# A constant tile multiplied ahead of the first data, and a last tile finished in two parts by two engines

## The chip, the cores and the metric

The kernel is one program on 1 core of one Trainium2 chip. Its metric is the device time of one execution in microseconds. The core has five engines that run side by side, each through its own list of instructions in order: TensorE (PE in the profile: matrix products; PEld are its weight loads), VectorE (DVE), ScalarE (ACT), GpSimd (POOL) and SyncE (SP), which here issues DMAs. They wait for each other through semaphores.

## The reference, cut to what matters

One layer of a decoder, on a prompt of 1024 rows of width 1024, and on eight single-row samples with a paged cache of 8192 positions. The sample group's work is spread between the prompt's. All data are float32.

```python
q, k, v, logf, u, z = mixer_inputs(rmsnorm(xp, g_mix[l]), w_in[l], b_f[l], g_sgu_v[l])
xp = xp + merge_heads(fox_prompt(q, k, v, logf), sgu_prompt(u, z, w_s[l], b_s[l]), g_att_out[l], g_sgu_out[l], w_o[l])
mk, mv = memory_kv(mem_prompt, g_mem[l], w_ck[l], w_cv[l])
xp = xp + cross_attend(rmsnorm(xp, g_cross[l]), mk, mv, w_cq[l], w_co[l])
f, conv_p = conv_ffn(rmsnorm(xp, g_ffn[l]), zeros, w_up[l], conv_w[l], conv_b[l], w_down[l])
xp = xp + f
...
y_prompt = rmsnorm(xp, g_final)
y_sample = rmsnorm(xs, g_final)

def rmsnorm(x, g):
    y = x * rsqrt(mean(x * x, axis=-1) + EPS)
    return y * g
```

What the change touches is the very start (before the first product of `mixer_inputs`) and the very end (`xp + f` and the final `rmsnorm` of the prompt's last 128 rows).

## The kernel before, in words

The prompt's 1024 rows are worked in two halves (`hf` 0 and 1) of 512, each as four tiles of 128 rows (`i` 0 to 3). A float32 product is made of three passes over operands split into a high and a low part of type float32r (`split`, lines 232 to 239: ACT writes the high part, DVE the rest): `gemm3` (lines 268 to 274) issues high times high, high times low, low times high. A plain float32 matmul (sample rows, transposes) goes without the split and is recorded as two or more passes.

**Order.** The program is written as generators whose steps are interleaved, and the Tile framework then places all instructions with a scheduler that runs a timeline model (`schedule_with_timeline_sim=True`, line 2003). So the order of an engine's list is the scheduler's: an instruction more at the start can move others far behind it. `tc.high_priority()` puts a step ahead of others that are ready.

**The start.** Constants are set by DVE (`ones`, `mhalf`, `epsb`, lines 180 to 185). SP issues the loads of `xT` and `w_in` (`load_x` line 388, `wload` line 252), four chunks of 256 of the contraction each, through four raw buffers (`wr`). In `p1` PE first multiplies the samples' rows by the raw weights (`sample_mm`, line 306), then the prompt's by the split ones (`by_rows`, lines 479 to 481), chunk by chunk. `MS()` (line 152) is one PSUM bank of its own.

**The end.** In `ffn` the down projection runs in groups of columns of the hidden width (`GROUPS`, 6, 6, 5, 5). Of the last group, for each half `n` of the 1024 output columns and each row tile `i`, `gemm3` makes 15 matmuls of 512 columns, and `residual` (line 1012) adds the result to `xt[i]` on DVE (line 1016) and sums its squares on ACT (`ssq_into`, line 230) into `sq[:, i, n]`. `final` (line 1346) then takes tile by tile: DVE adds the two halves' sums (line 1021) and scales them (222), POOL raises to the power -0.5 (223), DVE multiplies the tile by that factor and by `g_final` in one instruction (1353), SP issues the store to `o_y` (1354). The last tile of each half is multiplied and stored in two pieces of 512 columns.

Of the kernel before, what the change touches and what calls it, by code (L numbers as in the profile page):

```python
# [11 lines left out]
AF = mybir.ActivationFunctionType  # L12
ALU = mybir.AluOpType
# [5 lines left out]
P = 128  # L19
D = 1024  # L20
# [10 lines left out]
NF = FF // P  # L31
# [47 lines left out]
def build(nc, tc, ctx, a, phases=None):  # L79
# [27 lines left out]
    def nm(s):  # L107
        cnt[0] += 1
        return f"{s}_{cnt[0]}"
# [16 lines left out]
    def sm(shape, tag, bufs=2, dt=F32):  # L126
        return small.tile(shape, dt, tag=tag, bufs=bufs, name=nm(tag))
# [13 lines left out]
    def BB():  # L141
        return psum.tile([P, 512], F32, tag="bb", bufs=2 + MB, name=nm("bb"))
# [7 lines left out]
    MM = TR = BK  # L150

    def MS():
        return BB() if MB else psum.tile([P, 512], F32, tag="ms", bufs=1, name=nm("ms"))
# [11 lines left out]
    mmul = nc.tensor.matmul  # L165
# [14 lines left out]
    ones = const.tile([P, P], F32, tag="ones", name="ones")  # L180
    nc.vector.memset(ones, 1.0)
    mhalf = const.tile([P, 8], F32, tag="mhalf", name="mhalf")
    nc.vector.memset(mhalf, -0.5)
    epsb = const.tile([P, 1], F32, tag="epsb", name="epsb")
    nc.vector.memset(epsb, EPS)
    warm = const.tile([P, 1], F32, tag="warm", name="warm")
    nc.scalar.activation(warm, mhalf[:, 0:1], AF.Copy)
    bfb = const.tile([P, 8], F32, tag="bfb", name="bfb")
# [29 lines left out]
    def rstd_of(ssq, n, width, tag):  # L218

        p = ssq.shape[0]  # L220
        r = sm([P, width], tag + "r", 2)[:p]
        nc.vector.tensor_scalar(r, ssq, 1.0 / n, EPS, op0=ALU.mult, op1=ALU.add)
        nc.gpsimd.tensor_tensor(r, r, mhalf[:p, :width], op=ALU.pow)
        return r

    def ssq_into(dst, src):
        n = src.shape[-1]

        j = src if n > 512 else tpool.tile([P, 512], BF16, tag="junk", bufs=1, name=nm("junk"))[: src.shape[0], :n]
        nc.scalar.activation(j, src, AF.Square, accum_out=dst)  # L230
# [21 lines left out]
    def wload(src, n, raw=None):  # L252

        if raw is None:
            raw = wraw(src, n)
        l = spool.tile([P, SWID], F32R, tag="wl", bufs=WL, name=nm("wl"))[:, :n]
        h = spool.tile([P, SWID], F32R, tag="wh", bufs=WH, name=nm("wh"))[:, :n]
        if len(src.shape) == 3:
            h = h.rearrange("p (a b) -> p a b", b=src.shape[2])
            l = l.rearrange("p (a b) -> p a b", b=src.shape[2])  # L260
        split(raw, h, l)
        return h, l, raw
# [5 lines left out]
    def gemm3(out, pairs):  # L268

        n = len(pairs)  # L270
        for i, (sh, sl, mh, ml) in enumerate(pairs):
            mmul(out, sh, mh, start=(i == 0), stop=False)  # L272
            mmul(out, sh, ml, start=False, stop=False)  # L273
            mmul(out, sl, mh, start=False, stop=(i == n - 1))  # L274
# [734 lines left out]
    def squares():  # L1009
        return sm([P, 4, 2], "sqx", 2)  # L1010
# [8 lines left out]
    def rows_rstd(sq, i0, i1):  # L1019
        s = sm([P, i1 - i0], f"rq{i0}", 2)  # L1020
        nc.vector.tensor_tensor(s, sq[:, i0:i1, 0], sq[:, i0:i1, 1], op=ALU.add)
        return rstd_of(s, D, i1 - i0, f"rn{i0}")
# [238 lines left out]
    def ffn(hf, xt, ys, late=None):  # L1261
        begun = {ft: (wload(a["w_up"][ft], 1024), BK()) for ft in (0,)}

        def pairs(w, hs, ls, c):
            hv, lv = (w[q].rearrange("p (k c) -> p k c", c=P) for q in range(2))
            return [(hv[:, k, :], lv[:, k, :], hs[k][:, c], ls[k][:, c]) for k in range(8)]

        def first(hs, ls, c):
            gemm3_late([(pv[:, c], pairs(w, hs, ls, c)) for w, pv in begun.values()])

        hs, ls = yield from norm_T(ys, G_FFN, first)
        if hf:

            fix = sm([P, 2 * NF, 2], "fix", 1)
            tap = [gp[:, CW + i * 44 : CW + i * 44 + 44] for i in range(2)]
            for c in range(2):
                nc.vector.tensor_tensor(fix[:, :, c], hlast[0][:, :, 1], tap[1 - c], op=ALU.mult)
            t = sm([P, 2 * NF], "fixt", 1)
            nc.vector.tensor_tensor(t, hlast[0][:, :, 0], tap[0], op=ALU.mult)
            nc.vector.tensor_tensor(fix[:, :, 0], fix[:, :, 0], t, op=ALU.add)  # L1280
        sq = squares()
        f0 = 0
        for gi, gn in enumerate(GROUPS):
            gh, gl = [], []
            for f in range(f0, f0 + gn):
                hc2 = []
                for part in range(2):
                    ft = f + part * NF
                    cw = [gp[:, CW + i * 44 + ft : CW + i * 44 + ft + 1] for i in range(3)]
                    cb = gp[:, CB + ft : CB + ft + 1]  # L1290
                    if ft in begun:
                        pv = begun.pop(ft)[1]
                    else:
                        w_, pv = wload(a["w_up"][ft], 1024), BK()
                        gemm3(pv, pairs(w_, hs, ls, slice(0, 512)))
                    hc = T2()
                    nc.scalar.activation(hc, pv, AF.Identity, bias=cb, scale=cw[2])
                    nc.scalar.activation(hlast[hf][:, ft, :], pv[:, 510:512], AF.Copy)
                    nc.vector.scalar_tensor_tensor(hc[:, 1:], pv[:, :511], cw[1], hc[:, 1:], op0=ALU.mult, op1=ALU.add)
                    nc.vector.scalar_tensor_tensor(hc[:, 2:], pv[:, :510], cw[0], hc[:, 2:], op0=ALU.mult, op1=ALU.add)  # L1300
                    if hf:
                        nc.vector.tensor_tensor(hc[:, 0:2], hc[:, 0:2], fix[:, ft, :], op=ALU.add)
                    hc2.append(hc)
                    yield 5.2
                nc.scalar.activation(hc2[0], hc2[0], AF.Silu)
                nc.vector.tensor_tensor(hc2[1], hc2[1], hc2[0], op=ALU.mult)
                q = (f - f0) % 2
                if q == 0:
                    g2, l2 = U([P, 2, 512], F32R), U([P, 2, 512], F32R)
                split(hc2[1], g2[:, q, :], l2[:, q, :])  # L1310
                gh.append(g2[:, q, :])
                gl.append(l2[:, q, :])
            side = None
            if late and f0 + gn == NF:
                side = late()
            for n in range(2):
                ws = []
                for k2 in range(0, gn, 2):
                    m = min(2, gn - k2)
                    r0 = (f0 + k2) * P  # L1320
                    h, l, _ = wload(
                        a["w_down"][r0 : r0 + m * P, n * 512 : (n + 1) * 512].rearrange("(k p) n -> p k n", p=P), m * 512
                    )
                    for q in range(m):
                        ws.append((h[:, q, :], l[:, q, :]))
                for i in range(4):
                    tb = slice(i * P, (i + 1) * P)
                    ps = MM()
                    gemm3(ps[:, :512], [(gh[k][:, tb], gl[k][:, tb], ws[k][0], ws[k][1]) for k in range(gn)])
                    if f0 + gn < NF:  # L1330
                        xs_ = xt[i][:, n * 512 : (n + 1) * 512]
                        nc.vector.tensor_tensor(xs_, ps[:, :512], xs_, op=ALU.add)
                    else:
                        residual(xt, sq, i, n, ps)
                    yield 3.9
                    if side and n:

                        held[0] = True
                        for _ in range(2):
                            yield next(side)  # L1340
            f0 += gn
        if hf:
            nc.sync.dma_start(a["o_h"], hlast[1])
        return sq

    def final(hf, xt, sq):
        gf = U([P, D])
        nc.sync.dma_start(gf, a["g_final"].broadcast_to((P, D)))
        for i in range(4):
            r = rows_rstd(sq, i, i + 1)  # L1350
            rows = slice((hf * 4 + i) * P, (hf * 4 + i + 1) * P)
            for c in (slice(0, 512), slice(512, D)) if i == 3 else (slice(0, D),):
                nc.vector.scalar_tensor_tensor(xt[i][:, c], xt[i][:, c], r, gf[:, c], op0=ALU.mult, op1=ALU.mult)
                nc.sync.dma_start(a["o_y"][rows, c], xt[i][:, c])
        yield 1

    lastexp = []
    last = {}
    bgs, acc, phase = [], [0.0], ["p1", None]

# [664 lines left out]
```

## Time and profile before

| | |
|---|---|
| time, median of 3 runs | 1793.09 us (1792.41 to 1802.47) |
| the profiled execution, its own time | 1796.66 us |
| its span, first to last instruction | 1794.9 us |
| PE busy | 1736.6 us of the span, 9637 matmul records |
| DVE, ACT, POOL busy | 1399.3, 734.4, 496.1 us |
| moved by DMA | 521.07 MB, mean 290 GB/s |

The span is read along PE, which is busy nearly throughout: what counts are the stretches in which it is not, or in which its clock is low. Matmuls overlap in the records, so the pace is read from the distance of their starts, not from their durations.

### The profile page before, as it was taken

Reading aid. Unit: us, or ns where it says so; the run is one execution under the profiler, and the core shown is the slowest. Engines: PE = TensorE matmul, PEld = TensorE weight load, DVE = VectorE, ACT = ScalarE, POOL = GpSimd, SP = SyncE. Lnnn points to the kernel's source line nnn. Section 1 sums busy time; section 2 is a strip of 40 time slices with the busy share of each in tenths; the row PEclk is TensorE's granted clock in tenths of the full one; section 3 lists DMA queues with packets and bytes.
Section 4 is the critical chain, followed back from the end, with each engine's and each line's share of the span. In section 5 each row is a group of like instructions: output and inputs, shape, how many; then the busy total and the mean of one; then the engine's idle time right before and its main releaser. Section 6 shows DMA issues by size and latency. Waiting matters only on the chain.

```text
span 1794.9 us, 25099 instructions
## 1 busy us (share of the span) xinstructions
PE 1736.6 (97%) x9637; PEld 1286.9 (72%) x9637; DVE 1399.3 (78%) x1733; ACT 734.4 (41%) x1374; POOL 496.1 (28%) x461
## 2 busy tenths in 40 slices
PE   8999999889999999999999999999999999999997
PEld 5887777655677667777777777776676778767875
DVE  4689658988788987999999999887885549855344
ACT  6332256466643635333333244335353233333332
POOL 1252334432222332233322223333322122102110
PEclk9999999999999999999999999999999999999999
DMA  8886888787697975779788878978879687568982
GB/s 299 304 295 222 301 324 318 260 274 230 254 401 279 366 300 222 287 289 349 293 304 311 289 309 318 382 292 331 312 288 343 221 301 250 192 259 299 358 311 81
DMA packets 157075, 521.07 MB, mean 290 GB/s; under 512 B 20874, under 2 KB 40842, under 8 KB 124186
## 3 DMA queue, kind: packets, MB, share of 16 engines
q0 software_dynamic: 57168, 341.14, 50.2%
q1 hardware_dynamic: 92874, 165.73, 26.6%
q10 hardware_dynamic: 6912, 12.59, 1.9%
q8 instruction: 76, 1.25, 0.3%
q14 instruction: 45, 0.37, 0.1%
HBM read 495.47 MB, written 23.93 MB: 289 GB/s over the span
## 4 chain that ended last, share of the span: by engine, by line
PE 53%; DMA 9%; issue 8%; DVE 6%; POOL 2%; ACT 2%; POOLq 0%; DVEq 0%; ACTq 0%; SPq 0%
DMA kv<-cache_v,io 7%; PE ba L272 6%; PE ba L274 6%; PE ba L273 6%; PE dv L1488 4%; PE bb L272 3%; PE bb L273 3%; PE bb L274 3%; PE ba L1065 1%; PE ba L1064 1%; PE ba L1066 1%; PE dv L331 1%; DVE kv L1436 1%; PE dv L1764 1%; DVE s L1440 1%
## 5 line engine op out<-in xcount | busy, mean ns | idle before, releaser
L235 ACT ACTIVATE wh<-wr 128x1024 fp32r<-128x1024 f32 (+2 forms) x220 | 228.7, 1044 | 438.9 <-PE ba L273 152.7
L236 DVE TENSOR_TENSOR wl<-wr,wh 128x1024 fp32r<-128x1024 f32 (+2 forms) x220 | 263.0, 1200 | 165.7 <-PE ba L274 58.0
L1420 POOL DMA_INDIRECT kv<-cache_k,io x128 | 188.8, 1475 | 589.2 <-DVE s L1440 317.7
L1436 DVE TENSOR_TENSOR kv<-kv,d 128x1024 f32<-128x1024 f32 (+1 forms) x156 | 258.0, 1681 | 25.0 <-DMA kv<-cache_k,io 25.0
L1440 DVE TENSOR_REDUCE s<-kv 128x16 f32<-128x1024 f32 (+1 forms) x156 | 258.4, 1673 | 0.0
L1482 POOL DMA_INDIRECT kv<-cache_v,io x128 | 168.7, 1318 | 243.2 <-PE dv L1488 155.6
L272 PE MATMUL ba<-u,wh 128*128 128x512 f32 x528 | 209.8, 398 | 0.0
L273 PE MATMUL ba<-u,wh 128*128 128x512 f32 x528 | 208.8, 395 | 0.5 <-DVE u L239 0.5
L274 PE MATMUL ba<-u,wl 128*128 128x512 f32 x528 | 209.2, 397 | 0.0
L272 PE MATMUL ba<-wh,u 128*128 128x512 f32 (+1 forms) x495 | 186.1, 379 | 0.9 <-ACT u L235 0.9
L273 PE MATMUL ba<-wl,u 128*128 128x512 f32 (+1 forms) x495 | 185.3, 375 | 1.5 <-DVE wl L236 1.5
L274 PE MATMUL ba<-wh,u 128*128 128x512 f32 (+1 forms) x495 | 183.2, 375 | 0.0
L1488 PE MATMUL dv<-kv,s 128*32 128x512 f32 x1024 | 126.5, 600 | 4.6 <-DMA kv<-cache_v,io 4.6
L274 PEld LDWEIGHTS ba<-u,wl 128*128 128x128 f32 x528 | 99.5, 188 | 28.3 <-issue 5.7
L272 PEld LDWEIGHTS ba<-u,wh 128*128 128x128 f32 x528 | 99.6, 189 | 26.6 <-issue 4.8
L273 PEld LDWEIGHTS ba<-u,wh 128*128 128x128 f32 x528 | 99.6, 189 | 25.1 <-issue 2.3
L272 PEld LDWEIGHTS ba<-wh,u 128*128 128x128 f32 x495 | 93.0, 188 | 25.0 <-issue 6.5
L272 PE MATMUL bb<-u,wh 128*128 128x512 f32 x272 | 108.6, 399 | 0.0
L273 PE MATMUL bb<-u,wh 128*128 128x512 f32 x272 | 107.9, 397 | 0.1
L274 PE MATMUL bb<-u,wl 128*128 128x512 f32 x272 | 107.9, 397 | 0.0
L273 PEld LDWEIGHTS ba<-wl,u 128*128 128x128 f32 x495 | 93.1, 188 | 20.7 <-DVE wl L236 2.5
L274 PEld LDWEIGHTS ba<-wh,u 128*128 128x128 f32 x495 | 92.9, 188 | 19.4 <-issue 1.6
(451 smaller groups left out, 3311.9 us busy)
## 6 DMA issues: line engine op xcount, KB each, us to landing
wr<-w_up SPq DMA_DIRECT2D x88, 512.0 KB
kv<-w_up POOLq DMA_DIRECT2D x22, 1024.0 KB
wr<-w_down SPq DMA_DIRECT2D x40, 512.0 KB
kv<-w_down POOLq DMA_DIRECT2D x11, 1024.0 KB
wr<-w_in SPq DMA_DIRECT2D x16, 512.0 KB
wr<-w_o SPq DMA_DIRECT2D x16, 512.0 KB
wr<-w_cq SPq DMA_DIRECT2D x16, 512.0 KB
wr<-w_co SPq DMA_DIRECT2D x16, 512.0 KB
```

Source lines behind the costliest of these rows:

```text
L235: nc.scalar.activation(h, src, AF.Copy)
L236: nc.vector.tensor_tensor(l, src, h.bitcast(F32), op=ALU.subtract)
L272: mmul(out, sh, mh, start=(i == 0), stop=False)
L273: mmul(out, sh, ml, start=False, stop=False)
L274: mmul(out, sl, mh, start=False, stop=(i == n - 1))
L331: mmul(ps[32 * j : 32 * j + 32, :w], xT[:, k, :] if nk == 8 else xT[:, k * 8 : k * 8 + 32], raw[:, q, j * w : (j + 1) * w], start=(k == 0) ...
L1064: mmul(pss[i], mh[k][:, tb], wh, start=(k == korder[0]), stop=False)
L1420: nc.gpsimd.indirect_dma_start(kv, None, a["cache_k"], off(kidx[:, b, ch : ch + 1]))
L1436: nc.vector.tensor_tensor(kvv[:, i : i + m, :], kvv[:, i : i + m, :], qb.unsqueeze(1).broadcast_to((P, m, 512)), op=ALU.mult)
L1440: nc.vector.tensor_reduce(s[:, ch * 4 + i : ch * 4 + i + m, :].rearrange("p k h -> p (k h)"), kvv[:, i : i + m, :].rearrange("p k (h d) -> ...
L1482: nc.gpsimd.indirect_dma_start(kv, None, a["cache_v"], off(kidx[:, b, ch : ch + 1]))
L1488: mmul(dv[32 * j : 32 * j + 32, :], s[:, ch * 4 : ch * 4 + 4, :].rearrange("p k h -> p (k h)"), kvv[:, j, :], start=(ch == 1), stop=(ch == ...
```

## The change

It has two parts, in the lines below (numbers of the new file are 3 higher behind line 186, and 39 higher at the end).

1. Behind the constants, 13 float32 matmuls of the 128x128 tile `ones` with itself, into the PSUM bank of `MS()`. Nothing reads the result.
2. In the second half of the rows the last tile of the last group (`i == 3`, `n == 1`) goes to a new function `last_tile`: two products of 256 columns each, each with its own add and sum of squares, the mean and epsilon folded into ACT's instructions, so that DVE's two small steps fall away ahead of POOL's power. In `final`, tiles 2 and 3 of the second half are multiplied by two engines: columns 0 to 511 by `g_final` on DVE ahead of time and by the factor on ACT, columns 512 to 1023 by both on DVE; tile 3's first piece is stored from ACT's queue, the other pieces from SP's.

```diff
+    wm = MS()
+    for _ in range(13):
+        mmul(wm[:, :P], ones, ones, start=True, stop=True)
...
+        def last_tile(x, sq, pairs):
+            c2 = sm([P, 2], "lsq", 1)
+            part = sm([P, 2], "lpart", 1)
+            r3 = sm([P, 1], "lr", 1)
+            nc.scalar.activation(part[:, 0:1], sq[:, 3, 0:1], AF.Identity, scale=1.0 / D, bias=epsb)
+            for m in range(2):
+                ps = MM()
+                c = slice(m * 256, m * 256 + 256)
+                gemm3(ps[:, :256], [(sh, sl, mh[:, c], ml[:, c]) for sh, sl, mh, ml in pairs])
+                xs_ = x[:, 512 + m * 256 : 768 + m * 256]
+                with tc.high_priority():
+                    nc.vector.tensor_tensor(xs_, ps[:, :256], xs_, op=ALU.add)
+                    ssq_into(c2[:, m : m + 1], xs_)
+                    nc.scalar.activation(
+                        r3 if m else part[:, 1:2], c2[:, m : m + 1], AF.Identity, scale=1.0 / D, bias=part[:, m : m + 1]
+                    )
+            nc.gpsimd.tensor_tensor(r3, r3, mhalf[:, 0:1], op=ALU.pow)
+            lastr.append(r3)
...
+                    if hf and n and i == 3 and f0 + gn == NF:
+                        last_tile(xt[3], sq, [(gh[k][:, tb], gl[k][:, tb], ws[k][0], ws[k][1]) for k in range(gn)])
+                        continue
...
+            if hf and i > 1:
+                r = lastr[0] if i == 3 else rows_rstd(sq, i, i + 1)
+                for n, c in enumerate((slice(0, 512), slice(512, D))):
+                    if n:
+                        nc.vector.scalar_tensor_tensor(xt[i][:, c], xt[i][:, c], r, gf[:, c], op0=ALU.mult, op1=ALU.mult)
+                        nc.sync.dma_start(a["o_y"][rows, c], xt[i][:, c])
+                    else:
+                        nc.vector.tensor_tensor(xt[i][:, c], xt[i][:, c], gf[:, c], op=ALU.mult)
+                        nc.scalar.activation(xt[i][:, c], xt[i][:, c], AF.Copy, scale=r)
+                        (nc.scalar if i == 3 else nc.sync).dma_start(a["o_y"][rows, c], xt[i][:, c])
+                continue
```

The scheduler also places other instructions anew. On PE the order differs here and there from the 23rd row of its list to about the 3150th of 7049 (roughly the first 800 us), then not again until the last tile; DVE, ACT, POOL and SP likewise. Three places follow; names are those of the tiles (with the buffer's number), sizes are partitions by elements.

**PE at the start, before.** `wr` are raw weights, `xg` the samples' rows, `wh`, `wl` and `u` the split weights and rows.

```order
L2003 UNCONDITIONAL_BRANCH
L306 MATMUL ba_128<-wr_137,xg_108 32x512 x2
L479 MATMUL bb_275<-wh_140,u_131 128x512
L479 MATMUL ba_276<-wh_140,u_131 128x512
L479 MATMUL ba_277<-wh_140,u_131 128x512
L479 MATMUL bb_278<-wh_140,u_131 128x512
L480 MATMUL bb_275<-wl_139,u_131 128x512
```

And in the changed kernel:

```order
L2042 UNCONDITIONAL_BRANCH
L188 MATMUL ms_92<-ones 128x128 x13
L309 MATMUL ba_142<-wr_151,xg_122 32x512 x2
L482 MATMUL bb_289<-wh_154,u_145 128x512
L482 MATMUL ba_290<-wh_154,u_145 128x512
L482 MATMUL ba_291<-wh_154,u_145 128x512
L482 MATMUL bb_292<-wh_154,u_145 128x512
L483 MATMUL bb_289<-wl_153,u_145 128x512
```

The 13 new matmuls stand first; what follows them is as before. The samples' next pair, which stood three matmuls ahead of the end of the first chunk, now stands behind it.

**PE in the first half's attention, before** (scores `ba`: lines 807 to 811; transposes of weights `wr` by `cp`: line 836; values `bb_3775`: line 852).

```order
L852 MATMUL bb_3775<-u_3587,u_3212 64x256
L807 MATMUL ba_3809<-u_3566,u_3562 128x320
L809 MATMUL ba_3809<-u_3567,u_3562 128x320
L807 MATMUL ba_3809<-u_3566,u_3562 128x320
L809 MATMUL ba_3809<-u_3567,u_3562 128x320
L811 LDWEIGHTS ident_b
L811 MATMUL ba_3809<-cmask_b,ident_b 128x128
L836 MATMUL ms_3745<-cp,wr_3690 128x128 x4
L807 MATMUL ba_3828<-u_3566,u_3562 128x384
```

And now (lines 3 higher, buffers 14 higher):

```order
L855 MATMUL bb_3789<-u_3601,u_3226 64x256
L855 MATMUL bb_3789<-u_3691,u_3226 64x256
L855 MATMUL bb_3789<-u_3602,u_3226 64x256
L839 MATMUL ms_3810<-cp,wr_3747 128x128 x4
L810 MATMUL ba_3823<-u_3580,u_3576 128x320
L812 MATMUL ba_3823<-u_3581,u_3576 128x320
```

Of the value matmuls into that bank only one stood ahead of the two blocks of scores (`ba_3809`, `ba_3828`); now nine stand there, with groups of transposes between them.

**DVE and ACT at the end, before.** First DVE, then ACT; `u_9507` is tile 2, `u_9509` tile 3 (in the new file `u_9521` and `u_9523`).

```order
L1016 TENSOR_TENSOR u_9507<-ba_14727,u_9507 128x512
L1353 TENSOR_SCALAR u_9505<-u_9505,rn1r_14777,u_14766 128x1024
L1021 TENSOR_TENSOR rq_2654_14782<-sqx_11168 128x1
L222 TENSOR_SCALAR rn2r_14784<-rq_2654_14782 128x1
L1353 TENSOR_SCALAR u_9507<-u_9507,rn2r_14784,u_14766 128x1024
L1016 TENSOR_TENSOR u_9509<-bb_14746,u_9509 128x512
L1021 TENSOR_TENSOR rq_2656_14789<-sqx_11168 128x1
L222 TENSOR_SCALAR rn3r_14791<-rq_2656_14789 128x1
L1353 TENSOR_SCALAR u_9509<-u_9509,rn3r_14791,u_14766 128x512 x2
```

```order
L230 ACTIVATE junk_14669,sqx_11168<-u_9509 128x512
L230 ACTIVATE junk_14706,sqx_11168<-u_9503 128x512
L230 ACTIVATE junk_14725,sqx_11168<-u_9505 128x512
L230 ACTIVATE junk_14744,sqx_11168<-u_9507 128x512
L230 ACTIVATE junk_14763,sqx_11168<-u_9509 128x512
```

And now, DVE first:

```order
L1019 TENSOR_TENSOR u_9521<-ba_14741,u_9521 128x512
L1391 TENSOR_SCALAR u_9519<-u_9519,rn1r_14817,u_14806 128x1024
L1024 TENSOR_TENSOR rq_2660_14822<-sqx_11182 128x1
L1298 TENSOR_TENSOR u_9523<-bb_14764,u_9523 128x256
L225 TENSOR_SCALAR rn2r_14824<-rq_2660_14822 128x1
L1382 TENSOR_SCALAR u_9521<-u_9521,rn2r_14824,u_14806 128x512
L1298 TENSOR_TENSOR u_9523<-ba_14784,u_9523 128x256
L1382 TENSOR_SCALAR u_9523<-u_9523,lr_14762,u_14806 128x512
```

```order
L233 ACTIVATE junk_14758,sqx_11182<-u_9521 128x512
L233 ACTIVATE junk_14781,lsq_14760<-u_9523 128x256
L1300 ACTIVATE lpart_14761<-lsq_14760,lpart_14761 128x1
L1386 ACTIVATE u_9521<-u_9521,rn2r_14824 128x512
L233 ACTIVATE junk_14801,lsq_14760<-u_9523 128x256
L1300 ACTIVATE lr_14762<-lsq_14760,lpart_14761 128x1
L1386 ACTIVATE u_9523<-u_9523,lr_14762 128x512
L1387 DMA o_y<-u_9523 128x512
```

DVE's work of 1024 columns on tile 2 ahead of tile 3's add has become one of 512, and the two small steps behind that add are gone; ACT has three instructions between the two sums of squares and the store. The two multiplications by `g_final` (line 1385 of the new file) stand earlier in DVE's list.

More of the change, by code (lines that the diff above doesn't have):

```diff
@@ L1349, in final @@
         for i in range(4):
+            rows = slice((hf * 4 + i) * P, (hf * 4 + i + 1) * P)
+            if hf and i > 1:
[9 more added lines that the diff above has]
+                continue
             r = rows_rstd(sq, i, i + 1)
-            rows = slice((hf * 4 + i) * P, (hf * 4 + i + 1) * P)
             for c in (slice(0, 512), slice(512, D)) if i == 3 else (slice(0, D),):
@@ L1357, in build @@
     lastexp = []
+    lastr = []
     last = {}
```

## The prediction

> **What bounds the kernel now.** I read the page's first lines, then a table of PE's busy time in wide stretches, then the first 23 us and the last 13 us instruction by instruction, and last the stretches in which PE's clock is low.
>
> ```profile
> span 1794.9 us, 25099 instructions
> PE 1736.6 (97%) x9637; PEld 1286.9 (72%) x9637; DVE 1399.3 (78%) x1733; ACT 734.4 (41%) x1374; POOL 496.1 (28%) x461
> ```
>
> The table's first column behind the stretch is its length, then PE's busy time and matmul records, the other engines, PE's granted clock, the DMA share and GB/s.
>
> ```profile
> 0.00:100.00 100.00, 91.66 (x545) 74.63 (x546) 59.39 (x80) 47.04 (x72) 21.17 (x22) 1.00 0.81 297
> 300.00:800.00 500.00, 471.29 (x2631) 343.08 (x2630) 436.51 (x612) 249.27 (x524) 159.46 (x154) 0.99 0.80 290
> 1755.00:1794.90 39.90, 30.55 (x148) 22.95 (x140) 19.35 (x37) 8.74 (x24) 2.75 (x5) 0.93 0.18 68
> ```
>
> PE is the bound. Of its 58.3 us without a matmul (1794.9 - 1736.6), 8.3 lie in the first 100 us, 28.7 between 300 and 800, 9.4 in the last 40. The change can win at both ends; in between it can only shift waits. Matmul records overlap, so pace is the distance of starts. The start:
>
> ```profile
> 0.83 0.17 DVE L181 MEMSET ones<- 128x128 f32 x1 [0.83 <-PEq L2000]
> 7.10 1.92 PE L306 MATMUL ba<-wr,xg 128*32 128x512 f32 x4 [7.10 <-DMA wr<-w_in]
> 8.08 1.23 DVE L236 TENSOR_TENSOR wl<-wr,wh 128x1024 fp32r<-128x1024 f32 x1 [0.17 <-ACT wh L235]
> 8.95 0.80 PE L479 MATMUL bb<-wh,u 128*128 128x512 f32 x1
> 10.83 0.59 PE L480 MATMUL bb<-wl,u 128*128 128x512 f32 x1
> 11.25 0.40 PE L481 MATMUL bb<-wh,u 128*128 128x512 f32 x1
> 14.68 0.39 PE L481 MATMUL ba<-wh,u 128*128 128x512 f32 x1
> 15.00 1.05 PE L306 MATMUL ba<-wr,xg 128*32 128x512 f32 x4
> 18.66 1.41 DVE L239 SCALAR_TENSOR_TENSOR u<-wr,gp,u 128x512 fp32r<-128x512 f32 x2
> ```
>
> The first data release PE at 7.10. Two matmuls start 0.42 us apart (10.83 and 11.25), the 15 from there to 14.68 0.229 apart; the samples' pair takes 1.92 us at first and 1.05 later. PE runs at half pace for its first 4 us. (The clock column says 1.00 in the first 100 us although the pace doubles: there I trust the pace.)
>
> **Part 1, the constant tile.** Each new matmul is a float32 product of 128x128. The same form runs here in one row of 16 records, two for each of 8 instructions:
>
> ```profile
> 341.69 1.96 PE L649 MATMUL ba<-wr,u 128*128 128x128 f32 x16
> 343.40 0.36 PE L807 MATMUL ba<-u,u 128*128 128x256 f32 x1
> ```
>
> That is (343.40 - 341.69) / 8 = 0.214 us each at full pace, twice that, 0.43, at half. PE can start when `ones` is set, at about 1.05. Thirteen at half pace end at 1.05 + 5.6 = 6.6, before the data at 7.10: they cost nothing. If the clock rises as it did before, 4 us after PE's start, that is at about 5.1; 9 or 10 are slow, the rest end near 5.9.
>
> What it wins if the clock stays up: the pair runs 7.10 to 8.1; the four high-by-high matmuls end near 9.1; then PE waits for `wl`, ready at 8.08 + 1.23 = 9.31, and goes on at 9.35. Before, five prompt matmuls had started by 11.25, where full pace began; now four are done at 9.35. So PE is ahead by 11.25 - 9.35 - 0.229 = **1.67 us**. The next loads must keep up: the third chunk's last low part is ready at 18.66 + 1.41 = 20.07, and PE wants it after 44 matmuls and one pair, at 9.35 + 10.1 + 1.3 = 20.7, so 0.6 us of cover is left. The samples' second pair, now three matmuls later in the list, still ends at about 15.1 against 16.05 before, so the raw buffer it frees, and SP's weight load that waits for it, are not late. DVE, ACT and SP are not touched; later the evacuations and `wl` follow PE, so the lead is kept.
>
> **Does the clock stay up?** PE then idles from about 5.9 to 7.10, and 0.25 us for `wl`. Four stretches of 3.4 us:
>
> ```profile
> 366.26:369.67 3.41, 1.77 (x15) 1.22 (x16) 3.38 (x6) 2.85 (x8) 1.17 (x2) 1.00 1.07 401
> 376.49:379.90 3.41, 1.52 (x11) 1.05 (x10) 3.41 (x8) 2.92 (x7) 0.00 (x0) 1.00 0.11 31
> 379.90:383.31 3.41, 3.41 (x17) 3.10 (x17) 3.41 (x7) 1.83 (x6) 1.64 (x2) 0.50 0.02 2
> 1325.40:1328.80 3.40, 2.36 (x14) 0.94 (x6) 3.40 (x8) 1.58 (x4) 2.79 (x3) 1.00 1.05 383
> ```
>
> Behind stretches with PE busy 1.77 or 1.52 of 3.41 us (52%, 45%) the clock was 0.50 for one such stretch (third row); behind 2.36 of 3.40 (69%) it stayed. From a rise at 5.1 the next 3.41 us hold 1.2 us of idle time, so the share is 65%, nearer to the last row, so I take it that the clock stays. The Trainium skill ("TensorE: Matmul & The Clock Gate", Part 1) says the clock falls only after an idle window of about 3.4 us; by that a gap of 1.2 us is safe and the gain certain. The trace disagrees: half-idle windows were enough, so I keep the fall as a rival.
>
> **Part 2, the last tile.**
>
> ```profile
> 1777.92 0.69 DVE L1016 TENSOR_TENSOR u<-bb,u 128x512 f32<-128x512 f32 x1 [5.41 <-PE bb L274]
> 1781.80 8.63 SPq L1354 DMA_DIRECT2D o_y<-u  x5
> 1781.91 0.39 PE L272 MATMUL bb<-wh,u 128*128 128x512 f32 x1
> 1784.33 0.54 POOL L223 TENSOR_TENSOR rn2r<-rn2r,mhalf 128x1 f32<-128x1 f32 x1 [1.67 <-DVE rn2r L222]
> 1784.90 1.28 DVE L1353 SCALAR_TENSOR_TENSOR u<-u,rn2r,u 128x1024 f32<-128x1024 f32 x1 [0.65 <-POOL rn2r L223]
> 1785.15 0.40 PE L274 MATMUL bb<-wh,u 128*128 128x512 f32 x1
> 1786.11 0.68 DVE L1016 TENSOR_TENSOR u<-bb,u 128x512 f32<-128x512 f32 x1
> 1786.88 0.63 ACT L230 ACTIVATE junk<-u 128x512 bf16<-128x512 f32 x1 [3.27 <-DVE u L1016]
> 1787.42 0.19 ACT L230 ACTIVATION_READ_ACCUMULATOR junk<-u 128x1 f32 x1
> 1788.07 0.55 POOL L223 TENSOR_TENSOR rn3r<-rn3r,mhalf 128x1 f32<-128x1 f32 x1 [3.20 <-DVE rn3r L222]
> 1788.65 1.42 DVE L1353 SCALAR_TENSOR_TENSOR u<-u,rn3r,u 128x512 f32<-128x512 f32 x2 [0.66 <-POOL rn3r L223]
> ```
>
> Behind PE's last matmul (1785.55) the add waits until 1786.11 for DVE, busy with tile 2; then sum, two small steps, power, two multiplications, the last store at 1790.1. For the halves these rows give prices:
>
> ```profile
> 66.11 0.28 PE L274 MATMUL bb<-wh,u 128*128 128x260 f32 x1
> 66.23 0.28 PE L272 MATMUL bb<-wh,u 128*128 128x260 f32 x1
> L1646 DVE TENSOR_TENSOR dec<-dv,dec x6: 402/414/416, 1441.0 to 1765.1; 8x256 f32<-8x256 f32 x6
> L1185 ACT ACTIVATE cbs<-cmx,rq x32: 277/284/308, 581.5 to 1259.5; 128x1 f32<-128x1 f32 x32
> ```
>
> PE: 30 matmuls of 256 at 0.12 are 3.6 us for 15 at 0.229, 3.44; PE ends at about 1785.6, the first half near 1783.9. DVE adds that half (0.41) ahead of tile 2's small step, so tile 2's power moves from 1784.33 to about 1784.7 and ends at 1785.25; its multiplication of 512 columns (0.75, half of the 1.42) runs to 1786.0, the last add to 1786.45 instead of 1786.79. Sum of squares: about 0.52 with the readout (0.73 for 512 columns, less 0.21 for half of them), to 1787.0; ACT's step of one column 0.28, to 1787.3; the power from 1787.4 to 1787.95, where 1788.62 stood. Then the two engines multiply in parallel: both pieces are ready by 1788.73 (DVE, 0.75) and near 1788.6 (ACT, 0.63 for 512 columns), instead of 1789.37 and 1790.07. `g_final`'s multiplications on DVE ahead of time cost 0.7 us each in DVE's idle 5.4 us before 1777.9, on no path. Tile 2's two stores stand ahead of tile 3's on SP and are issued by 1786.3.
>
> The stores (the last two columns are the DMA share and GB/s):
>
> ```profile
> 1790.00:1791.00 1.00, 0.00 (x0) 0.00 (x0) 0.06 (x1) 0.00 (x0) 0.00 (x0) 0.50 0.72 274
> 1791.00:1791.50 0.50, 0.00 (x0) 0.00 (x0) 0.00 (x0) 0.00 (x0) 0.00 (x0) 0.50 1.03 393
> 1791.50:1792.00 0.50, 0.00 (x0) 0.00 (x0) 0.00 (x0) 0.00 (x0) 0.00 (x0) 0.50 0.29 107
> ```
>
> 274 x 1.0 + 393 x 0.5 + 107 x 0.5 is 524 KB, both pieces of the last tile, moved without a gap to about 1791.65: the second waited for the first's bytes, not for DVE alone. So what counts is when the first piece is ready, near 1788.6 instead of 1789.37: **0.76 us** won. If the second piece alone counted, it would be 1790.07 - 1788.73 = 1.34; if ACT's and DVE's steps on the half tile cost as much as on a whole one, some 0.4. I take 0.76, the row's reading. The Trainium skill ("DMA: Bandwidth & Descriptors", Issuing engines are not separate DMA queues) says that DMAs from several engines share the same 16 DMA engines and save only issue time. That speaks against storing from ACT's queue too, and agrees with these rows; by it the term is 0.76, without it 1.34.
>
> **Part 3, the new order up to about 800 us.** Nothing is added there but moves. One place where it matters:
>
> ```profile
> 403.35 0.42 PE L807 MATMUL ba<-u,u 128*128 128x320 f32 x1 [0.68 <-ACT wr L817]
> 406.27 0.45 PE L807 MATMUL ba<-u,u 128*128 128x384 f32 x1 [1.53 <-ACT wr L817]
> ```
>
> PE waits there 0.68 and 1.53 us for ACT to empty a score bank. Now eight value matmuls stand ahead of both. If they were ready, they would fill 2.2 us; but they read what ACT and DVE write behind a transpose that now stands just ahead of them, so they may wait as long themselves. I count zero. Bounds: a low-clock stretch costs 3.41 / 2 = 1.7 us, and the idle time that sets it off 3.41 - 1.77 = 1.6; one such event more or less is 3.3 us. PE idles 28.7 us between 300 and 800, so I allow one or two events either way, about -4 to +6.
>
> **Sum.** 1.67 + 0.76 = 2.43 us, of 1796.66 for the profiled execution (span 1794.9 and 1.76 around it), that is 1794.2. That execution lies 3.57 above the median of 1793.09; against the median the forecast is **1790.7 us**.
>
> **The rivals.**
>
> *The clock falls again in the gap.* For it: if the clock rises early, say at 4.5, eight matmuls are slow and five fast, PE is done by 5.6, idles 1.5 us plus 0.25 at 9.1, and a stretch that holds most of it is 50 to 56% busy, close to the 52% that sufficed. Against: 69% did not, and the phase of these stretches decides. Then the prompt's matmuls are slow from about 8 to 11.3, as before, and only the tail is won: 1793.09 - 0.76 = 1792.3.
>
> *The new order costs: slower than before.* The mechanism is one: in the first half's attention PE waits for ACT's evacuations, and a wait that leaves a 3.4 us stretch half idle halves the clock for the next. For it: two such drops lie between 366 and 384 in the rows above already, and PE's order differs most from here to 620 us. Against: as many waits can vanish. It decides from 2.4 us on, so one new event of 3.3 us suffices: 1790.7 + 3.3 = 1794.0; two give 1797.3.
>
> *The new order wins.* The same the other way: 2.2 us of waits at 403 to 406 and the 1.7 us of one low-clock stretch gone give 1790.7 - 3.9 = 1786.8.
>
> *The tile does nothing.* If a product of ones did not raise the clock, 1792.3 again; nothing in this trace shows a matmul whose operands matter, so I put it into the first rival.
>
> **How the numbers follow.** Forecast 0.43; clock falls or never rises 0.19; order costs 0.23; order wins 0.15. The range of 8 in 10 runs from the winning order with the tail's upper bound (1786.8 - 0.6, about 1786) to two events (1797.3). All cases lie within 7 us of the median; 1%, about what a measurement of this kernel can tell from no change, is 18 us. That would need five or six events of one sign: 0.02 for each side, 0.96 for within 1%.
>
> **What would show it.** Right: 26 records of line 188 between about 1.05 and 6 us, the first samples' pair at 7.10 taking about 1.0 us instead of 1.92, prompt matmuls 0.23 us apart from the first on, a wait for `wl` ending near 9.35, PE 1.7 us ahead near 23 us. In the tail: 30 matmuls of 256 columns, POOL's last power ending about 2.35 us behind PE's last matmul instead of 3.07, the last bytes moved 2.95 us behind that. Wrong: starts 0.42 us apart again between 8 and 11 us; the first data later than 7.10 because PE is still busy; tile 2's multiplication on ACT holding up the last sum of squares; or a lead that is gone by 800 us, with PE idle more than 28.7 us from 300 to 800 or more low-clock stretches there.

## The result, and the profile after

| | before | changed |
|---|---|---|
| median of 22 runs each, us | 1794.87 (1789.87 to 1802.47) | 1800.03 (1793.89 to 1808.37) |
| ratio, 95% interval | | 1.0027 (1.0017 to 1.0037) |
| profiled execution, span | 1794.9 | 1796.7 |

The changed kernel is 0.27% slower, some 5 us, where 2.4 us less were forecast. The two profiled executions lie only 1.8 us apart, so the profiles show where time goes, and the ratio says what the change costs. The page's first lines after, and the three wide stretches:

```profile
span 1796.7 us, 25196 instructions
PE 1741.0 (97%) x9678; PEld 1288.8 (72%) x9678; DVE 1398.6 (78%) x1733; ACT 734.1 (41%) x1381; POOL 486.4 (27%) x461
```

```profile
0.00:100.00 100.00, 96.70 (x578) 80.06 (x579) 60.40 (x81) 46.81 (x72) 21.36 (x22) 1.00 0.82 299
300.00:800.00 500.00, 468.73 (x2609) 337.97 (x2608) 429.94 (x604) 246.29 (x523) 154.99 (x153) 0.98 0.79 286
1755.00:1796.70 41.70, 33.34 (x190) 25.51 (x188) 20.30 (x37) 12.69 (x32) 2.73 (x5) 0.94 0.18 66
```

PE idles 31.3 us from 300 to 800 us instead of 28.7, at a lower mean clock. The start and the end went nearly as forecast. First PE's timeline at the start, then the last steps:

```profile
1.05 5.69 PE L188 MATMUL ms<-ones 128*128 128x128 f32 x26 [1.05 <-DVE mhalf L183]
7.21 1.05 PE L309 MATMUL ba<-wr,xg 128*32 128x512 f32 x4 [0.48 <-DMA wr<-w_in]
9.46 0.50 PE L483 MATMUL bb<-wl,u 128*128 128x512 f32 x1
9.80 0.40 PE L484 MATMUL bb<-wh,u 128*128 128x512 f32 x1
10.04 0.40 PE L483 MATMUL ba<-wl,u 128*128 128x512 f32 x1
```

```profile
1788.07 0.28 PE L277 MATMUL ba<-wh,u 128*128 128x256 f32 x1
1789.87 0.54 POOL L1303 TENSOR_TENSOR lr<-lr,mhalf 128x1 f32<-128x1 f32 x1 [2.07 <-ACT lr L1300]
1790.44 0.72 ACT L1386 ACTIVATE u<-u,lr 128x512 f32<-128x512 f32 x1 [0.65 <-POOL lr L1303]
1790.45 0.75 DVE L1382 SCALAR_TENSOR_TENSOR u<-u,lr,u 128x512 f32<-128x512 f32 x1 [1.52 <-POOL lr L1303]
```

The samples' pair takes 1.05 us instead of 1.92, and the prompt's matmuls follow at 0.24 us instead of 0.42. From PE's last matmul to the end of the span are 8.35 us (1796.7 - 1788.35) instead of 9.35 (1794.9 - 1785.55). So the loss lies between. The steps in which the samples' values are multiplied (16 matmul records each, lines 1488 and 1527) stand in the same sequence in both kernels and serve as milestones:

| start of the same step, us: before | changed | behind (+) |
|---|---|---|
| 566.38 | 565.98 | -0.4 |
| 599.25 | 603.23 | +4.0 |
| 647.01 | 652.91 | +5.9 |
| 1200.50 | 1205.58 | +5.1 |
| 1405.71 | 1408.45 | +2.7 |

6.3 us go between 566 and 653. (Up to 566 us the distance swings both ways, 3.4 us behind at the step at 361.54 and 3.9 ahead at that at 489.61, and is back near zero. Some 2.3 of the 6.3 come back in these two executions near 1250 and 1340 us; near 1250 before's has the longer wait for a page, 3.29 us against 2.82, and a mean clock of 0.91 against 1.00.) PE's waits from 470 to 656 us, where the columns are the total, how many and the longest; before, then after:

```profile
PE ba L1180 <- ACT t L1167: 1.4, 1, 1.4
...
PE dv L1488 <- DMA kv<-cache_v,io: 0.2, 1, 0.2
```

```profile
PE dv L1527 <- DMA kv<-cache_v,io: 5.7, 3, 2.5
PE ba L1183 <- ACT t L1170: 1.1, 1, 1.1
```

PE now waits for pages of the value cache, which GpSimd gathers. The longest wait, in PE's timeline, and two windows of 2 us around it (PE busy first behind the length, then PEld, DVE, ACT, POOL, the granted clock, DMA share, GB/s):

```profile
583.50 3.44 PE L1527 MATMUL dv<-kv,s 128*32 128x512 f32 x16 [2.47 <-DMA kv<-cache_v,io]
```

```profile
582.00:584.00 2.00, 0.50 (x4) 0.20 (x8) 0.00 (x0) 0.00 (x0) 0.00 (x0) 0.80 0.99 367
584.00:586.00 2.00, 2.00 (x12) 0.39 (x8) 0.00 (x0) 0.00 (x0) 0.26 (x1) 0.50 1.05 428
```

2.47 us of waiting, then the step itself at half clock: 3.44 us, where it takes 1.92 elsewhere. Together 4.0. Why the pages came late is seen on GpSimd and VectorE. GpSimd's gathers before and after, then VectorE's list beside them:

```profile
567.75 1.00 POOL L1482 DMA_INDIRECT kv<-cache_v,io  x1 [5.69 <-PE dv L1488]
569.06 0.95 POOL L1482 DMA_INDIRECT kv<-cache_v,io  x1 [0.30 <-PE bb L274]
```

```profile
567.35 0.96 POOL L1521 DMA_INDIRECT kv<-cache_v,io  x1 [6.25 <-PE dv L1527]
568.62 6.67 POOL L1521 DMA_INDIRECT kv<-cache_v,io  x1 [0.30 <-PE bb L277]
```

```profile
568.99 1.21 DVE L1440 TENSOR_REDUCE s<-kv 128x16 f32<-128x1024 f32 x1
```

```profile
568.65 2.34 DVE L1475 TENSOR_TENSOR kv<-kv,d 128x1024 f32<-128x1024 f32 x2
570.91 1.21 DVE L239 TENSOR_TENSOR wl<-wr,wh 128x1024 fp32r<-128x1024 f32 x1
572.05 0.14 DVE L1503 TENSOR_TENSOR mT<-m,snT 8x1 f32<-8x1 f32 x1
572.12 2.34 DVE L239 TENSOR_TENSOR wl<-wr,wh 128x1024 fp32r<-128x1024 f32 x2
574.39 2.33 DVE L1479 TENSOR_REDUCE s<-kv 128x16 f32<-128x1024 f32 x2
```

Before, the second gather is issued beside a VectorE sum (one input) and takes 0.95 us. After, it is issued as VectorE begins six operations one behind the other, each with two inputs in SBUF, and ends at 575.29: 0.90 us behind the start of the first operation with one input. The moved order put the two together.

### The profile page after: what moved, and what is told of

It is laid out like the page before. It is cut to its first block, busy times and chain, and to the rows that moved or that the text cites. A ratio compares the mean times of both kernels' runs of the same rounds, so it can differ in the third digit from the quotient of the medians.

```text
span 1796.7 us, 25196 instructions
## 1 busy us (share of the span) xinstructions
PE 1741.0 (97%) x9678; PEld 1288.8 (72%) x9678; DVE 1398.6 (78%) x1733; ACT 734.1 (41%) x1381; POOL 486.4 (27%) x461
## 4 chain that ended last, share of the span: by engine, by line
PE 50%; DMA 8%; issue 7%; DVE 6%; POOL 2%; ACT 1%; POOLq 0%; DVEq 0%
PE ba L275 7%; PE ba L277 7%; PE ba L276 7%; DMA kv<-cache_v,io 7%; PE dv L1527 4%; PE bb L276 3%; PE bb L275 3%; PE bb L277 3%; DVE s L1479 1%; PE dv L334 1%; PE ba L1068 1%; PE ba L1069 1%; PE dv L1803 1%; PE ba L1067 1%; DVE wl L239 1%
## 5 line engine op out<-in xcount | busy, mean ns | idle before, releaser
L1459 POOL DMA_INDIRECT kv<-cache_k,io x128 | 177.5, 1386 | 584.8 <-DVE s L1479 317.6
L275 PE MATMUL ba<-wh,u 128*128 128x512 f32 (+2 forms) x500 | 187.7, 378 | 0.9 <-ACT u L238 0.9
L276 PE MATMUL ba<-wl,u 128*128 128x512 f32 (+2 forms) x500 | 186.6, 374 | 1.5 <-DVE wl L239 1.5
L277 PE MATMUL ba<-wh,u 128*128 128x512 f32 (+2 forms) x500 | 184.7, 375 | 0.0
```

Source lines behind the costliest of these rows:

```text
L1459: nc.gpsimd.indirect_dma_start(kv, None, a["cache_k"], off(kidx[:, b, ch : ch + 1]))
```

## The experiments

Three theories at first. *Order*: the instructions that the scheduler moved cost 6 to 7 us. *Head*: the constant products themselves cost later. *Tail*: the new last tile costs. A build with five constant products or fewer keeps before's order of all other instructions; from six on the scheduler gives the order of the changed kernel. A section of their own (`tc.tile_critical`) around the products keeps before's order too.

**Only the new last tile** (`wm` and its loop taken out of the changed kernel).

```diff
-    wm = MS()
-    for _ in range(13):
-        mmul(wm[:, :P], ones, ones, start=True, stop=True)
```

> Only the new last tile; no constant products, and every engine's order before the last tile is the one of before. Order theory (the moved instructions between about 500 and 640 us cost 6 to 7 us, the constant products and the new last tile win what was forecast): 0.8 us faster than before, ratio about 0.9996, and PE's lag against before within 2 us of zero from 100 to 1780 us except where low-clock stretches fall elsewhere. Head theory (the constant products themselves cost, by the clock or by what they hold up): the same, 0.9996. Tail theory (the new end costs): slower, by up to the whole 4.9 us, ratio up to 1.003.

Measured: 1.0004 (0.9992 to 1.0016). In the trace the end after PE's last matmul is 8.35 us, as in the changed kernel. The tail does not cost; its gain of 1 us is too small for these ratios.

**The moved order with too few products.**

```diff
+    wm = MS()
+    for _ in range(6):
+        mmul(wm[:, :P], ones, ones, start=True, stop=True)
```

> Six constant products instead of thirteen and the old last tile: the instructions behind them stand in the same moved order as in the changed kernel, but at half pace the six end near 3.6 us, 3.5 us ahead of the first data, so the clock is hardly raised. Order theory: no gain at the head, the loss stays, 6 to 7 us slower than before, ratio 1.0033 to 1.004, PE falling back by 4 us or more between 500 and 640 us. Head theory (thirteen products, or the clock that they raise, cost later): with less than half of them and no raised clock the loss shrinks, ratio 1.000 to 1.0015. Tail theory: 1.000.

Measured: 1.0040 (1.0023 to 1.0057). The gather of value pages near 569 us and PE's step behind it:

```profile
569.18 6.67 POOL L1485 DMA_INDIRECT kv<-cache_v,io  x1 [0.30 <-PE bb L277]
```

```profile
584.04 2.46 PE L1491 MATMUL dv<-kv,s 128*32 128x512 f32 x16 [2.45 <-DMA kv<-cache_v,io]
```

The gather takes 6.67 us again, PE waits 2.45 us, and at 652.88 it is 5.9 us behind before, as in the changed kernel. The order costs without a raised clock: the head theory falls as the cause of the loss.

**The products in before's order.**

```diff
+    wm = MS()
+    with tc.tile_critical():
+        for _ in range(9):
+            mmul(wm[:, :P], ones, ones, start=True, stop=True)
```

> Nine constant products in a section of their own, which keeps every instruction behind them in before's order (one branch more on each engine; PE starts them only when the first small transfer is in, about 3 us, so at half pace they end near 6.9 us); old last tile. Order theory: the head's gain alone, 1.3 to 1.7 us faster than before, ratio 0.9991 to 0.9993, no fall-back between 500 and 640 us. Head theory: slower, 4 to 6 us, ratio 1.002 to 1.0035. Tail theory: about 0.9992.

Measured: 1.0013 (0.9997 to 1.0028). No fall-back between 500 and 640 us, but no gain either: a miss for the order theory's number. Where the lead goes is seen at the second block of weights. PE's timeline of this run, then of the changed kernel, then of before:

```profile
56.61 1.08 PE L310 MATMUL bb<-wr,xg 128*32 128x512 f32 x8
58.80 1.05 PE L310 MATMUL bb<-wr,xg 128*32 128x512 f32 x4 [1.07 <-DMA wr<-w_in]
60.48 1.05 PE L310 MATMUL bb<-wr,xg 128*32 128x512 f32 x4 [0.58 <-DMA wr<-w_in]
63.34 0.39 PE L277 MATMUL ba<-wl,u 128*128 128x260 f32 x1 [0.72 <-DVE wl L240]
```

```profile
56.56 1.08 PE L309 MATMUL bb<-wr,xg 128*32 128x512 f32 x8
59.26 1.05 PE L309 MATMUL bb<-wr,xg 128*32 128x512 f32 x4 [0.66 <-DMA wr<-w_in]
62.12 0.39 PE L276 MATMUL ba<-wl,u 128*128 128x260 f32 x1 [0.72 <-DVE wl L239]
```

```profile
57.95 1.08 PE L306 MATMUL bb<-wr,xg 128*32 128x512 f32 x8
59.79 1.05 PE L306 MATMUL bb<-wr,xg 128*32 128x512 f32 x4
62.66 0.39 PE L273 MATMUL ba<-wl,u 128*128 128x260 f32 x1 [0.73 <-DVE wl L236]
```

Both come to this block 1.3 to 1.4 us ahead and wait for `w_in`; behind it 0.5 us are left in the changed kernel, and this run is 0.7 us behind before. (This execution, 1792.96 us, is the fastest of its 12, whose median is 1796.85. So the trace shows where the lead goes, but not what the slower executions lose; that stays open.) From 28 to 56 us the DMA engines have no gap in any of the three (changed kernel):

```profile
28.00:56.00 28.00, 28.00 (x120) 21.87 (x119) 5.18 (x10) 14.71 (x26) 10.15 (x10) 1.00 1.03 414
```

**Both parts in before's order** (the run before with the new last tile).

> The run before with the new last tile as well: the whole change without the moved order. Order theory: 2.1 to 2.5 us faster than before, ratio 0.9986 to 0.9988, and faster than the changed kernel by 6 to 7 us. Head theory: slower than before by 3 to 5 us, ratio 1.002 to 1.003. Tail theory: slower by 3 to 5 us too.

Measured: 0.9998 (0.9984 to 1.0012). Without the moved order the whole change costs nothing, and wins nothing that the ratio shows (the forecast lies inside the interval).

Now the cause within the order. *Port theory*: a gather that GpSimd issues waits until VectorE's run of operations with two inputs in SBUF has a gap. It was tested by one VectorE instruction more, put ahead of the products of one page of keys; PE's, GpSimd's and SyncE's orders stay those of the changed kernel; in VectorE's and ACT's lists a few neighbours of the sum change places.

**One needless sum, one input.**

```diff
             m = 4 // sp
+            gap = {(3, 1): 2}.get((b, ch))
+            if gap:
+                with behind(ENG.DVE):
+                    nc.vector.tensor_reduce(
+                        s[:, ch * 4 : ch * 4 + gap, :].rearrange("p k h -> p (k h)"),
+                        kvv[:, :gap, :].rearrange("p k (h d) -> p (k h) d", d=64),
+                        axis=AX.X,
+                        op=ALU.add,
+                    )
```

> The changed kernel with one needless VectorE sum of 128x1024 put ahead of the products of sample 3's second page of keys; the sum reads the page alone and its result is written over later. No other engine's order moves but two of ACT's. Port theory (the gather that GpSimd issues there takes 6.67 us because VectorE runs operations with two inputs in SBUF one behind the other; the sum has one input and lets the gather through): the second gather of values near 568.6 us takes about 0.95 us, its pages land in time, PE's wait of 2.47 us near 583.5 and the low-clock stretch behind it go, 3 to 4 us faster than the changed kernel although VectorE has 1.2 us more to do; ratio to before 1.0003 to 1.0012, and PE's lag against before at 650 us about -2 instead of -5.9. Rival (the pages are late because the three weight loads of 512 KB issued at 572.5 to 574.9 take the DMA engines, or because the page's key work is late): the issue stays near 6.67 us or the wait near 583.5 stays, ratio 1.0027 to 1.0035.

**The same with two inputs.**

```diff
-                    nc.vector.tensor_reduce(
...
+                    nc.vector.tensor_tensor(kvv[:, :gap, :], kvv[:, :gap, :], kvv[:, :gap, :], op=ALU.max)
```

> As the run before, with the same order on every engine, but the needless operation of 128x1024 is a maximum of the page with itself, which has two inputs in SBUF. Port theory: the gather near 568.6 us now waits through one more operation, 7.2 to 8 us instead of 6.67, PE's wait near 583.5 grows to 3 us or more; ratio to before 1.0027 to 1.004. Rival (what counts is that VectorE's work starts 1.2 us later, not its inputs): the same as the run before, whatever that shows.

GpSimd's gathers with one input, then with two:

```profile
570.76 0.95 POOL L1530 DMA_INDIRECT kv<-cache_v,io  x1 [0.30 <-PE bb L277]
572.02 6.54 POOL L1459 DMA_INDIRECT kv<-cache_k,io  x1 [0.30 <-DVE s L1476]
```

```profile
570.18 7.80 POOL L1525 DMA_INDIRECT kv<-cache_v,io  x1 [0.30 <-PE bb L277]
```

PE's step behind them, in the same sequence:

```profile
583.10 1.92 PE L1536 MATMUL dv<-kv,s 128*32 128x512 f32 x16
```

```profile
585.06 3.47 PE L1531 MATMUL dv<-kv,s 128*32 128x512 f32 x16 [2.47 <-DMA kv<-cache_v,io]
```

The two programs differ in one operation, at the same place and 1.2 us long in both (the sum also writes less, 16 values a partition against 1024; the last section tells the two apart). With one input the gather takes 0.95 us (the next one, for keys, takes the stall), and PE's wait and the half clock are gone; with two it takes 7.80, as the theory said, and PE waits. From the step at 566 us to that at 599 the run with one input loses 0.3 us on before (568.12 to 601.31 against 566.38 to 599.25), the one with two 4.4 (567.54 to 604.80), the changed kernel 4.4. Ratios: 1.0013 (0.9995 to 1.0031) and 1.0030 (1.0017 to 1.0044). These intervals overlap, so it is the traces that tell the two runs apart, not their times. Two misses: the first is a little above its range, since at 652.64 it is 5.6 us behind before and not 2 (it was 1.7 behind at the step at 566 us already, and its next steps wait for ACT and for one later page; from 566 to 653 it loses 3.9 us, the changed kernel 6.3); and PE's wait in the second stayed 2.47.

**Two sums in the changed kernel**: `gap = {(3, 1): 2, (7, 4): 4}`, the second where a gather of values takes 4.30 us near 1239.

> The changed kernel with two needless one-input VectorE sums: the one of 128x1024 ahead of sample 3's second page of keys (as in the run with one sum) and one of 128x2048 ahead of sample 7's fifth, where a gather of values takes 4.30 us near 1239 us and PE then waits 2.82 us near 1253.6. Port theory: both gathers take about 0.95 us (the second perhaps 2, where an operation with two inputs is already running), the waits near 583 and 1253 go or fall below 1 us; about 6 us faster than the changed kernel, ratio to before 0.9985 to 1.0000. Rival (late pages have another cause): 1.002 to 1.0035.

Measured: 0.9993 (0.9977 to 1.0008). The second gather fell to 2.00 us, PE's waits for value pages from 8.8 us to 2.6 over the whole span. So with two needless instructions the ratio is back at before's. That is not the moved order's cost alone, though: the second sum removes a stall that before's order has too (4.29 us, shown next), and before with sums of this kind is faster still (0.9983, the last of the next three).

Before's order has stalled gathers too:

```profile
771.92 4.83 POOL L1482 DMA_INDIRECT kv<-cache_v,io  x1 [0.30 <-issue]
1234.10 4.29 POOL L1482 DMA_INDIRECT kv<-cache_v,io  x1 [1.59 <-PE dv L1488]
```

PE waits 1.12 us at 781.8 and 3.29 at 1249.0. The sums there are `gap = {(4, 5): 4, (7, 4): 4}`.

**With products, new last tile and both sums, in before's order.**

> Nine constant products in a section of their own and the new last tile, in before's order, with two needless VectorE sums of 128x2048 with one input: ahead of the products of sample 4's sixth and of sample 7's fifth page of keys, where gathers of values took 4.80 us (near 769.7 us) and 4.30 us (near 1234.3). Port theory: both gathers take about 0.95 us, PE's waits of 1.73 us at 780 and 3.10 us at 1249 go or fall below 0.5; 4 to 6 us faster than the same kernel without the sums, ratio to before 0.996 to 0.9975. Rival (other transfers make these pages late): the waits stay, ratio 0.9985 to 1.0005.

**The same without the products.**

> As the run before without the constant products: the new last tile and the two sums, in before's order. Port theory: the waits of 1.91 us at 782 and 3.56 us at 1248 go, ratio to before 0.9965 to 0.998. If the head's lead of 1.3 us is lost near 59 us, where PE then waits for w_in, this run is as fast as the run before it within 1 us; if it is kept, 1.3 to 1.7 us slower. Rival: 0.999 to 1.0005.

**The kernel before with nothing but the two sums.**

> The kernel before with nothing but the two needless sums of 128x2048 (ahead of the products of sample 4's sixth and sample 7's fifth page of keys); PE's, GpSimd's and SyncE's orders are those of before. Port theory: PE's waits of 1.12 us at 781.8 and 3.29 at 1249.0 go or fall below 1 us, 2.5 to 4.5 us faster than before although VectorE has 4.5 us more to do, ratio 0.9975 to 0.9986. Rival: 0.9995 to 1.0015. Against the run with the new last tile and the same sums it should be 0.5 to 1 us slower, if the last tile wins 0.8.

Measured, in this order: 1.0000 (0.9987 to 1.0013), 0.9989 (0.9976 to 1.0002), 0.9983 (0.9971 to 0.9996). The gathers of the last one, and PE's wait for value pages over the whole span before and in it:

```profile
772.55 0.93 POOL L1491 DMA_INDIRECT kv<-cache_v,io  x1 [0.31 <-issue]
...
1232.80 1.34 POOL L1491 DMA_INDIRECT kv<-cache_v,io  x1 [1.06 <-PE dv L1497]
```

```profile
PE dv L1488 <- DMA kv<-cache_v,io: 4.6, 3, 3.3
```

```profile
PE dv L1497 <- DMA kv<-cache_v,io: 0.2, 1, 0.2
```

The kernel before becomes faster, by 0.17% (the interval ends close to 1, at 0.9996), with 4.5 us more of VectorE's work; it beats both kernels. The other two lie above their ranges. In their profiles the waits did fall (none near 781 us, 0.94 and 1.0 us near 1242), but the kernel with the products has no better ratio than without the sums (1.0000 and 0.9998), against the 4 to 6 us expected, while the one without the products has (0.9989 and 1.0004, with intervals that overlap). So no lasting gain of the products is shown here, and what else their section costs stays open.

**A later start.** Does the DMA alone set the pace up to 60 us? `range(9)` became `range(22)` in the section of its own.

> Before's order and last tile, and 22 constant products in place of 9 in the section of their own, so that PE turns to the first data only near 10.1 us, 2.4 us later than with 9, at full clock. If the transfers set the pace up to 60 us (theory of the lost lead), PE is about 1 us behind before at 25 us and the 9-product run 1.3 us ahead of it, but from 65 us on the two lie within 0.5 us of each other, near -0.6. If PE's own work sets the pace (the prediction's step), the 2.3 us between them stay to 100 us.

One execution, of 1804.21 us. The pair started at 10.89 instead of 7.68, and PE was 1.9 us behind before at 25 us, 3.2 behind the run with 9 products. From 65 us on it was 2.4 behind before and 1.8 behind that run. So neither: a lead is lost at the weights, but of a delay a good half stays. The raw buffer that the pair frees may be why: the load behind it was issued at 11.98 us, with 9 products at 11.16, before at 10.92. That was not tried by itself.

## Why the prediction was wrong

**The constant tile, part 1: right up to 56 us.** The products ran 1.05 to 6.74, at half pace until near their end: ten records took the last 2.11 us, so the clock rose later than at 5.1. At 7.21 it was up, as the pair's 1.05 us show, and the wait for `wl` ended at 9.46 (forecast 9.35). By the prediction's own sum the lead was 11.25 - 9.46 - 0.229 = 1.56 us instead of 1.67, and 1.39 were there at the pair near 57 us (57.95 - 56.56). The step that failed is "later the evacuations and `wl` follow PE, so the lead is kept". The prediction had followed the loads to 20.7 us only. The next block of `w_in` stands behind transfers that fill the DMA engines from 28 to 56 us, and PE waits for it: against before, 0.5 us were left behind it. (The later start shows that the transfers are not the whole cause.) Against the run with six products, which has the moved order without the raised clock, more was left: the same step starts at 275.11 us in the changed kernel and at 276.82 there, but a later one at 364.91 and 365.02. So in these executions the lead is lost in both orders, in the moved one only behind 300 us, at a place that was not looked for. The rival of a falling clock did not occur; it was hardly put to the test, since PE idled 0.48 us ahead of the pair and not 1.2.

**The last tile, part 2: right, a little small.** The last power ended 2.06 us behind PE's last matmul (forecast 2.35, before 3.07), and the end came 1.0 us sooner (forecast 0.76, with 1.34 as the upper bound).

**The new order, part 3: this is where it went wrong.** "Nothing is added there but moves ... I count zero." The run with six products has this order alone, with the old end and no raised clock, and is 0.40% slower, some 7 us; the changed kernel, with both gains, 0.27%, some 5. In the changed kernel's profile 6.3 us go from 566 to 653 us, 4.4 of them up to 603: the stalled gather, PE's wait for its pages and the half clock behind it. One of the prediction's own signs of being wrong is there, PE idle 31.3 us from 300 to 800 us. The rival "the new order costs" had the sign and the form (a wait, then a stretch at half clock; 3.3 us for one event, measured 4.0), but named the wrong wait and place: ACT's evacuations in the first half's attention. There the orders traded places without a lasting loss (the step at 544.16 us before starts 2.1 us sooner after). The loss was in waits for value pages behind 566 us, of which before has 0.2 us there. The read that could have found it is the gathers' durations, 0.94 us at the least and 4.29 or 4.83 at the two places where PE waited for values, held against VectorE's list, whose new order was known. Of the remaining 1.9 us up to 653 us most is a second late value page: the step at 633.26 us waits 1.75 us for it (before's 0.24), 13.5 us behind the issue of its last gather, which took 0.96 us. PE's waits for ACT are the same there (2.0 us in both kernels), and so nearly is the DMA share from 600 to 640 us (0.91, before 0.92). Why that page is late was not tried and stays open.

**The range.** Its top, 1797.3, stood on two events; and the base, a median of three, was 1793.09 where 22 runs have 1794.87.

## What to carry over

Where a scheduler places the instructions, six small matmuls at the start can move waits 500 us away: build a variant that keeps the old order (here five products, or a section of their own) and measure the edit and the order apart. A lead at the start is worth only what is left of it further on: here it went near 60 us, where PE waited for weights, or some 300 us later. And where one engine issues the gathers, read how long each issue takes: a stall there appeared here as another engine's DMA wait some 10 us later.

## What was not expected of the hardware

A gather's issue on GpSimd is held up by VectorE's operations with two inputs in SBUF, often through several of them one behind the other. Of the 264 gathers of before 87 took 1.2 us or more, 111 us beyond 0.95 each in sum; in 55 of these 87 the duration less its overlap with such operations is 0.78 to 0.95 us, about what an undisturbed issue takes. All but one of the 87 have such an operation beside them, and 85 end 0.77 to 0.96 us behind the end of one, 14 of these while the next of its kind was already running (the one of 4.29 us among them). Of the 97 gathers with none beside them the longest took 1.24 us. Among these are 25 beside operations with one input in PSUM and one in SBUF, which write 128 to 512 values a partition, and they took 1.03 us at most: so the two inputs in SBUF count, not a wide result. Not every gather is held up: of 117 that were issued while such an operation ran, 35 took less than 1.2 us. The gathers of keys and of values by groups (busy sum, mean ns):

```profile
L1420 POOL DMA_INDIRECT kv<-cache_k,io x128 | 188.8, 1475 | 589.2 <-DVE s L1440 317.7 <-PE dv L1488 135.2 <-DVE s L1428 41.6
L1482 POOL DMA_INDIRECT kv<-cache_v,io x128 | 168.7, 1318 | 243.2 <-PE dv L1488 155.6 <-DVE s L1440 41.4 <-issue 18.8
```

The Trainium skill ("SBUF — State Buffer", Who interferes with whom) says that a `tensor_reduce` never contends with GpSimd, and that a `tensor_tensor` with both inputs in SBUF contends with GpSimd's reads but was not seen to stall a DMA. The runs agree on the first (0.95 us beside a sum) and differ on the second for these gathers (6.67 and 7.80 us beside `tensor_tensor` alone); they read their row numbers (`io`) from SBUF, so what it says of GpSimd's reads covers them.
